# The boundary between two layers of a trunk kernel: a norm's sums, spread and use behind different products, the first pair's gate taken forward, keys and queries side by side

## The chip, the cores and the metric

The kernel runs on one core of a Trainium2 chip. Such a core has five engines that run at the same time, each through its own row of instructions in order, and wait for each other by semaphores: TensorE (PE in the profile, with PEld for its weight loads) does matrix products, VectorE (DVE), ScalarE (ACT) and GpSimd (POOL) work on tiles, and SyncE (SP) here issues the transfers between memory and the on-chip buffers. The metric is the device time of one execution in microseconds (us); shown is the median of the runs, beside a traced execution with the time of every instruction.

## The reference

The trunk has two layers. Each normalizes its input by rows, scales and shifts it by values computed from a condition `c`, runs a mixer, and adds the result times a gate. Layer 0's mixer is differential attention beside a recurrent unit; layer 1's is an attention in a window of a 16 x 64 grid, with 16 heads. The sequence has 1024 tokens of width 1024, one batch, all in fp32.

```python
def rms_norm(x, g):
    y = xf * lax.rsqrt(jnp.mean(xf * xf, axis=-1, keepdims=True) + EPS)
    return (y * g.astype(jnp.float32)).astype(x.dtype)
...
def odd_mixer(h, w_in, w_out, rpb):
    proj = h @ w_in
    q, k, v, g = jnp.split(proj, 4, axis=-1)
    out = neighborhood_attention(q.reshape(shp), k.reshape(shp), v.reshape(shp), rpb)
    return (out * jax.nn.silu(g)) @ w_out
...
    for l in range(DEPTH):
        mod = c_act @ ada_w[l] + ada_b[l]
        shift, scale, gate = jnp.split(mod, 3, axis=-1)
        h = rms_norm(x, norm_g[l]) * (1.0 + scale[:, None, :]) + shift[:, None, :]
        ...
        x = x + gate[:, None, :] * y
    return rms_norm(x, final_g)
```

## The kernel before

**Layout.** Activations stand transposed: channels on the partitions (8 tiles of 128, index `k` or `c`), tokens along the free axis, in two halves of 512 (`hf`). A product of fp32 numbers is made of three fast ones (`mm3`, L195 to L197): each operand is split into a high and a low part, and high x high, low activations x high weights and high activations x low weights are added up in PSUM (as the profile names them, L195, L196, L197).

**Weights.** They come in slabs of 1024 x 128, numbered in the order of use. SP loads a slab (`raw`, L152), ACT copies its high part (`whi`, L179), POOL subtracts for the low part (`wlo`, L180). `split_next` issues these two and then the load of the next slab, whose buffer comes free when the subtraction is done; `ahead(i)` does so early for slab `i`. `proj` (one product) takes a slab and one half: 24 matmuls, three for each `k`, the low weights first in the third. It yields after every two `k`, so that other work can be put between.

**The boundary.** `out_layer` with layer 0 makes the output projection, slabs 24 to 31 for the first half of the tokens and 32 to 39 for the second (`run`). Behind each slab an evacuation on DVE adds gate times product to x (L963), SP writes the sum to memory for later (L966), ACT squares it (L968) and DVE adds the square up (L974). `tail` then makes the norm: `ss_add` (L321) sums over the channels by 4 matmuls with ones, `rstd_rows` (L331 to L337) makes the reciprocal root on DVE in 11 steps, `spread` (L350) lays it out over all partitions (tile `bc`) by 4 matmuls, and `make_h` makes the next layer's input of each tile: L360 on DVE, the high part on ACT (L361), the low part on DVE (L362). For the first half the sums and the spread stood within the second half's products. For the second half the sums were made in two sets: of the first seven squares added up, and of the eighth.

Then come the first products of layer 1, head pair 0: keys (slab 40) and queries (slab 41), each for both halves, then values (slabs 42 and 43) and, among the attention's work, the gate (slab 44). Their evacuations are `evac_k` (L568 to L571), `evac_q` (L584 to L591, with two transfers that duplicate queries) and `evac_g1`, which takes tanh on ACT (L605) and multiplies on DVE (L606).

**Attention.** 64 units (8 pairs of heads, 2 halves, 4 blocks) go through three stages in a pipeline: `na_a` (logits `n`, L600 and L601; bias and maximum on DVE, L1162; exponential on ACT, L1165; division on POOL, L1170), `na_b` (transposes `etr`, L1182, copied by ACT and DVE, L1186 and L1188) and `na_c` (products with values, `no`, L1206). The projections of later pairs are fed in between by a feed that counts matmul time. The values of two pairs are made as a product of tokens x channels (`v`, L195 to L197, 128x256), copied out (`vt`), written to memory (`vd`, L1069) and read back in the window's order (`vc`, L1081). The bias of a unit is loaded by `load_bias` (L1137).

**Modulations.** The `c @ ada_w` rows for later use are made on DVE in between: `ada` pieces come by SP (L291), and L293 and L295 multiply and add them (`macc`). In layer 1 their buffers have the tag `tmp`, three in number, which the gate tiles `sg1` use too.

**What sets the order.** The program is written as generators that are advanced step by step (`some(gen, n)`); a list scheduler then orders the instructions of each engine by priority and readiness as it models them. `tc.high_priority()` takes instructions ahead, `tc.issue_after(x)` holds them behind instruction x. A tile that is allocated where another one lies waits for the last use of that one. SP is one queue in order for all loads and stores.

## Time and profile before

| quantity | value |
|---|---|
| median of 3 runs | 1241.4 us (1240.64 to 1245.04) |
| profiled execution, its time | 1242.87 us |
| its span (first to last instruction) | 1240.7 us |
| mean granted clock of PE | 0.983 of full speed |
| out projection of layer 0 to the last values' write | about 520 to 680 us |

"L12" is line 12 of the kernel's file. A row of a timeline has a start, a duration, engine, line, operation, output <- inputs and how many instructions it groups; in square brackets stands how long the engine stood idle before it and what ended that. A list of waits has the total, the number and the longest. The windows give busy time and count of each engine in a stretch. [...]

### The profile page before, as it was taken

The page shows a single profiled execution, that of the slowest core. Times are in us where ns is not written, and L with a number is a line of the kernel's source. Part 1 is how long each engine was busy: PE and PEld are TensorE (multiplying, and loading weights), DVE is VectorE, ACT ScalarE, POOL GpSimd, SP SyncE. Part 2 cuts the span into 40 slices and gives each one's busy share as a digit, 9 for nine tenths or more (in the row PEclk, how much of TensorE's full clock was granted, in tenths as well). Part 3 has the DMA queues.
Part 4 walks back from the last instruction along what each step waited for, and adds up shares of the span by engine and source line. Part 5 has one row for each costly group of instructions (what it writes and reads, how often), then busy time and mean ns, then how long its engine had stood idle before and what let it go on. Part 6 is the DMA issues. An engine that isn't in the chain of part 4 may idle for free.

```text
span 1240.7 us, 19096 instructions
## 1 busy us (share of the span) xinstructions
PE 1186.4 (96%) x7240; PEld 975.0 (79%) x7240; DVE 727.5 (59%) x1417; ACT 552.9 (45%) x1023; POOL 373.8 (30%) x348
## 2 busy tenths in 40 slices
PE   4989999899999999999999899999999999999997
PEld 3578877778888887777779689888988898877896
DVE  6753966798899889678561443353233324464344
ACT  4337658365656556423352333343243334465211
POOL 2114422133333325433322233233333333324100
PEclk8999999899999999999999899999999999999998
DMA  9511153222132201384433343333332333323312
GB/s 333 184 34 45 41 178 94 97 71 92 30 105 61 83 18 51 107 291 153 144 112 102 126 124 112 109 119 105 103 101 79 102 98 116 85 70 107 144 68 69
DMA packets 81467, 132.24 MB, mean 107 GB/s; under 512 B 7008, under 2 KB 48096, under 8 KB 81376
## 3 DMA queue, kind: packets, MB, share of 16 engines
q1 hardware_dynamic: 81376, 131.03, 33.6%
q8 instruction: 57, 0.93, 0.3%
q14 instruction: 34, 0.28, 0.1%
HBM read 110.03 MB, written 14.68 MB: 101 GB/s over the span
## 4 chain that ended last, share of the span: by engine, by line
PE 78%; DVE 10%; DMA 4%; issue 3%; ACT 2%; SPq 1%; POOL 1%; DVEq 0%; ACTq 0%; POOLq 0%
PE pp L195 15%; PE pp L197 15%; PE pp L196 15%; PE no L1206 4%; PE etr L1182 3%; PE v L195 2%; PE v L196 2%; PE atr L858 2%; PE v L197 2%; PE n L600 2%; PE n L601 2%; PE s L600 2%; PE s L601 2%; DMA vd<-vt 1%; DVE e L828 1%
## 5 line engine op out<-in xcount | busy, mean ns | idle before, releaser
L195 PE MATMUL pp<-ahi,whi 128*128 128x512 f32 (+1 forms) x1040 | 409.1, 394 | 3.3 <-DVE sgb L606 3.3
L197 PE MATMUL pp<-ahi,wlo 128*128 128x512 f32 (+1 forms) x1040 | 400.0, 385 | 0.8 <-POOL wlo L180 0.8
L196 PE MATMUL pp<-alo,whi 128*128 128x512 f32 (+1 forms) x1040 | 398.7, 384 | 0.0
L180 POOL TENSOR_TENSOR wlo<-raw,whi 128x1024 fp32r<-128x1024 f32 x80 | 195.6, 2447 | 332.8 <-ACT whi L179 332.8
L195 PEld LDWEIGHTS pp<-ahi,whi 128*128 128x128 f32 x1040 | 198.2, 191 | 46.3 <-issue 9.4
L197 PEld LDWEIGHTS pp<-ahi,wlo 128*128 128x128 f32 x1040 | 198.1, 190 | 39.7 <-POOL wlo L180 1.2
L196 PEld LDWEIGHTS pp<-alo,whi 128*128 128x128 f32 x1040 | 198.3, 191 | 33.4 <-issue 1.1
L179 ACT ACTIVATE whi<-raw 128x1024 fp32r<-128x1024 f32 x80 | 84.3, 1055 | 132.3 <-PE pp L196 84.1
L1162 DVE CUSTOM_DVE_ANT_0 e<-n,bias 128x288 f32<-128x288 f32 (+1 forms) x128 | 60.2, 505 | 141.2 <-PE n L601 75.3
L1170 POOL TENSOR_SCALAR e<-e,r 128x288 f32<-128x288 f32 (+1 forms) x128 | 70.1, 560 | 193.8 <-DVE r L1168 186.9
L1165 ACT ACTIVATE e<-e,nm 128x288 f32<-128x288 f32 (+1 forms) x128 | 72.8, 570 | 109.6 <-DVE nm L1162 108.9
L832 ACT ACTIVATE e<-e,nm 128x1024 f32<-128x1024 f32 x64 | 73.4, 1148 | 38.3 <-DVE nm L828 37.6
L828 DVE CUSTOM_DVE_ANT_0 e<-s,tb 128x1024 f32<-128x1024 f32 x64 | 76.9, 1217 | 4.0 <-DMA tb<-in_tb_dram 2.1
L196 PE MATMUL v<-wlo,ahi 128*128 128x256 f32 x256 | 72.5, 283 | 2.7 <-POOL wlo L180 2.7
L195 PE MATMUL v<-whi,ahi 128*128 128x256 f32 x256 | 74.7, 292 | 0.0
L197 PE MATMUL v<-whi,alo 128*128 128x256 f32 x256 | 72.3, 282 | 0.0
L295 DVE SCALAR_TENSOR_TENSOR macc<-ada,ctmp,macc 128x512 f32<-128x512 f32 x56 | 47.6, 851 | 28.7 <-DMA ada<-in_adaw_dram 28.3
L849 POOL TENSOR_SCALAR e<-e,r 128x256 f32<-128x256 f32 x32 | 32.9, 1027 | 100.6 <-DVE r L838 42.5
L1186 ACT ACTIVATE et<-etr 96x384 f32<-96x384 f32 (+1 forms) x64 | 31.2, 488 | 68.9 <-DVE et L1188 64.3
L1206 PE MATMUL no<-et,vc 96*64 96x128 f32 (+1 forms) x768 | 60.6, 282 | 0.0
L1206 PEld LDWEIGHTS no<-et,vc 96*64 96x64 f32 (+1 forms) x768 | 42.2, 136 | 21.6 <-issue 19.9
L963 DVE SCALAR_TENSOR_TENSOR xh<-pp,mod,xh 128x512 f32<-128x512 f32 (+1 forms) x40 | 25.6, 642 | 56.8 <-PE pp L197 49.5
(206 smaller groups left out, 2000.0 us busy)
## 6 DMA issues: line engine op xcount, KB each, us to landing
raw<-in_w_dram SPq DMA_DIRECT2D x56, 512.0 KB
ada<-in_adaw_dram SPq DMA_DIRECT2D x96, 256.0 KB
raw<-in_wo_dram SPq DMA_DIRECT2D x24, 512.0 KB
bias<-in_nab_dram SPq DMA_DIRECT2D x32, 288.0 KB
qq<-qq SPq DMA_DIRECT2D x48, 128.0 KB
bias<-in_nab_dram SPq DMA_DIRECT2D x16, 384.0 KB
xT<-in_xT_dram SPq DMA_DIRECT2D x16, 256.0 KB
xh<-in_xTp_dram SPq DMA_DIRECT2D x16, 256.0 KB
```

The lines of the kernel that those rows point to most:

```text
L179: A.activation(hi[:], raw[:], AF.Copy)
L180: G.tensor_tensor(lo[:], raw[:], hi[:], ALU.subtract)
L195: T.matmul(ps, lh, rh, start=start, stop=False)
L196: T.matmul(ps, lh, rl, start=False, stop=False)
L197: state["pe"] = T.matmul(ps, ll, rh, start=False, stop=stop).ins
L600: T.matmul(dst, qsel(q[m]), k, start=True, stop=False)
L828: state["dve"] = V.tensor_tensor_reduce(out=e[:], in0=ps[:].rearrange("p a b -> p (a b)"), in1=tbt[h][:, o:o + S], scale=-1.0, scalar=3.0e ...
L832: A.activation(e[:], e[:], AF.Exp, scale=-1.0, bias=nm[:], accum_out=sums[:, m:m + 1])
L1162: state["dve"] = V.tensor_tensor_reduce(out=e[:, m, :n], in0=ps[:, m, :n], in1=bias["now"][:, m, :n], scale=-1.0, scalar=3.0e38, op0=ALU.a ...
L1165: A.activation(e[:, m, :n], e[:, m, :n], AF.Exp, scale=-1.0, bias=nm[:, m:m + 1], accum_out=sums[:, m:m + 1])
L1170: state["pool"] = G.tensor_scalar(e[:, m, :n], e[:, m, :n], r[:, m:m + 1], 0.0, ALU.mult, ALU.add).ins
L1206: T.matmul(po[64 * m:64 * m + 64, b * P:(b + 1) * P], vch[p, b][:kn, j + hf, 64 * m:64 * m + 64], et[:kn, m, j * P:(j + 1) * P], start=(j ...
```

## The change

1. In `tail`, the sums and the spread are each held behind the last product that was issued before them (`issue_after(state["pe"])`). There is one more stop between `rstd_rows` and `spread`, so that another product can stand there. For layer 0 the eighth square is added on DVE and the second half has one set of sums.
2. The gate of pair 0 is made in the boundary, behind keys and queries of the first half. Slab numbers change: 42 is the gate, 43 and 44 the values. Its weights lie in buffers of `mixp[1]`, its tanh tiles in the boundary's pool `bp` under tag `sq`.
3. Order of the boundary: keys, first half; sums of the second half; queries, first half; spread; gate, first half, with `make_h` of the second half in between; keys and queries of the second half side by side, in pieces of six matmuls; gate, second half. The slabs are split earlier by more calls of `ahead`.

```diff
+        if i == at1["g", 0]:
+            pool, tags = mixp[1], ("mix6", "mix7")
...
-    def rstd_bc(ss, n, pool, bc):
-        spread(rstd_rows(ss, n, pool), bc)
...
-        order1 += vs + kq if p else kq + vs
-        if p < NA_PAIRS - 2:
+        order1 += vs + kq if p else kq + [("g", 0)] + vs
+        if 0 < p < NA_PAIRS - 2:
             order1.append(("g", p))
...
-                    last = s == len(segments) - 1
+                    last = l and s == len(segments) - 1
...
                 sums[s] = ss_start(f"ssl{l}_{s}")
-                ss_add(sums[s], acc[s], True, True, w)
+                with tc.issue_after(state["pe"]):
+                    ss_add(sums[s], acc[s], True, True, w)
+            if xdst is None:
+                rr = rstd_rows_act(sums[s], D, pool, w)
+            else:
+                rr = rstd_rows(sums[s], D, pool)
+                yield
             bc = ptp.tile([P, HF], F32, tag="pt", name=f"bc{l}_{s}")
-            if xdst is None:
-                spread(rstd_rows_act(sums[s], D, pool, w), bc, w)
-            else:
-                rstd_bc(sums[s], D, pool, bc)
+            with tc.issue_after(state["pe"]):
+                spread(rr, bc, w)
...
+    def evac_g1(p, pool, tag="sq", late=False):
+        def f(hf, ps):
+            c = slice(hf * HF, (hf + 1) * HF)
+            t = pool.tile([P, HF], F32, tag=tag, name="sg1", bufs=3)
+            ...
+                if hf == 0:
+                    mix_tile(p, f"sg1_{p}")
+                silu2(hf, ps, t, mixed[p][:, c])
...
         for c in range(KC):
             some(r1, 1)
-            some(t0, 2)
+            some(t0, (1, 1, 2, 2, 2, 2, 0, 0)[c])
         t1 = tail(1, to_h1)
+        ev = {"k": evac_k(("b", 0)), "q": evac_q(("b", 0)), "g": evac_g1(0, bp)}
+        first = lambda key, hf: proj(at1[key, 0], hf, ev[key], prep=False)
+        ahead(at1["q", 0])
+        some(first("k", 0), 99)
         some(t1, 1)
-        k0, q0 = evac_k(("b", 0)), evac_q(("b", 0))
-        for i, (key, hf, ev) in enumerate((("k", 0, k0), ("q", 0, q0), ("k", 1, k0), ("q", 1, q0))):
-            for _ in proj(at1[key, 0], hf, ev, prep=(i == 0)):
-                pass
-            some(t1, (3, 5, 0, 0)[i])
-        ahead(at1["q", 0] + 1)
+        ahead(at1["g", 0])
+        some(first("q", 0), 99)
+        some(t1, 1)
+        for _ in first("g", 0):
+            some(t1, 2)
+        k1, q1 = first("k", 1), first("q", 1)
+        for _ in range(5):
+            some(k1, 1)
+            some(q1, 1)
+        ahead(at1["g", 0] + 1)
+        some(first("g", 1), 99)
+        ahead(at1["g", 0] + 2)
...
-                t = ap.tile([P, HF], F32, tag="tmp", name="sg1", bufs=3)
...
+        feed.done.add("1g0")
...
-            if p < NA_PAIRS - 2:
-                feed.add(f"1g{p}", both(at1["g", p], evac_g1(p)))
+            if 0 < p < NA_PAIRS - 2:
+                feed.add(f"1g{p}", both(at1["g", p], evac_g1l(p)))
```

Lines below 340 shift by two, those of the attention by about 20: `mm3` is L197 to L199 now, the split L181 and L182, `spread` L352.

The first place is on PE, at the first half's spread (`bc0_0`). The names give slab and half of the product (`pp33_1` is slab 33, second half of the tokens), the activations' tile and the weights' parts. Before, it stood within slab 33's product:

```order
L195 MATMUL pp33_1_5303<-ahi1_1_4851,whi33_5266 128x512
L196 MATMUL pp33_1_5303<-alo1_1_4852,whi33_5266 128x512
L350 MATMUL bc0_0_5277<-rr_5279,sel_93 128x128 x4
L197 MATMUL pp33_1_5303<-ahi1_1_4851,wlo33_5267 128x512
L195 MATMUL pp33_1_5303<-ahi2_1_4855,whi33_5266 128x512
```

Now:

```order
L198 MATMUL pp33_1_5293<-alo3_1_4860,whi33_5266 128x512
L199 MATMUL pp33_1_5293<-ahi3_1_4859,wlo33_5267 128x512
L352 MATMUL bc0_0_5329<-rr_5278,sel_93 128x128 x4
L197 MATMUL pp34_1_5336<-ahi4_1_4831,whi34_5323 128x512
L198 MATMUL pp34_1_5336<-alo4_1_4832,whi34_5323 128x512
```

The spread moved from behind the 17th to behind the 24th matmul of slab 33. The second half's sums likewise stood within slab 39's and slab 40's products, its spread behind the 22nd matmul of slab 40; now the sums stand between slabs 40 and 41, the spread between slabs 41 and 42.

The second place is on POOL, the subtractions of the boundary's slabs. Before (40 keys, 41 queries, 42 and 43 values, 44 gate):

```order
L180 TENSOR_TENSOR wlo40_5603<-raw40_5567,whi40_5602 128x1024
L180 TENSOR_TENSOR wlo41_5659<-raw41_5606,whi41_5658 128x1024
L180 TENSOR_TENSOR wlo43_5860<-raw43_5811,whi43_5859 128x1024
L180 TENSOR_TENSOR wlo42_5808<-raw42_5662,whi42_5807 128x1024
L180 TENSOR_TENSOR wlo44_5932<-raw44_5863,whi44_5931 128x1024
```

Now (42 gate, 43 and 44 values):

```order
L182 TENSOR_TENSOR wlo40_5595<-raw40_5562,whi40_5594 128x1024
L182 TENSOR_TENSOR wlo42_5657<-raw42_5604,whi42_5656 128x1024
L182 TENSOR_TENSOR wlo41_5601<-raw41_5598,whi41_5600 128x1024
L182 TENSOR_TENSOR wlo43_5840<-raw43_5660,whi43_5839 128x1024
L182 TENSOR_TENSOR wlo44_5874<-raw44_5843,whi44_5873 128x1024
```

The gate's slab stands ahead of the queries' one, though the queries' product comes first on PE.

The third place is on SP, behind the boundary. Before, the last block of the values (`vd_83`) stood here, with only one `ada` load of layer 1 ahead of all value blocks:

```order
L152 DMA raw47_6330<-in_w1_dram 128x1024
L1069 DMA vd_83<-vt_6134 8x16x256
L152 DMA raw48_6485<-in_w1_dram 128x1024
L1081 DMA vc0_2_6147<-vd_83 128x1x128 x2
L1081 DMA vc0_3_6152<-vd_83 96x1x128 x2
L291 DMA ada_6206<-in_adaw_dram 128x512
L1137 DMA bias_6274<-in_nab_dram 128x2x384
L291 DMA ada_6271<-in_adaw_dram 128x512
```

Now, the first blocks of the values:

```order
L1157 DMA bias_5889<-in_nab_dram 128x2x288
L1157 DMA bias_5891<-in_nab_dram 128x2x384
L293 DMA ada_5998<-in_adaw_dram 128x512
L152 DMA raw47_6252<-in_w1_dram 128x1024
L1097 DMA vd_83<-vt_5950 8x16x256
L1157 DMA bias_6001<-in_nab_dram 128x2x288
L293 DMA ada_6268<-in_adaw_dram 128x512
L293 DMA ada_6334<-in_adaw_dram 128x512
L1097 DMA vd_83<-vt_5988 8x16x256
L1157 DMA bias_6271<-in_nab_dram 128x2x288
L293 DMA ada_6419<-in_adaw_dram 128x512
L1109 DMA vc0_0_6197<-vd_83 96x1x128
```

Four `ada` loads stand ahead of the first read of the values. The first two bias loads, which before stood ahead of slab 44's load, now stand behind slab 46's; the first of them waits for the gate's last multiply on DVE, since its tile lies where the boundary's pool was.

## The prediction

> **What bounds the kernel now.** I read the busy shares first, then the chain that ended last, the waits of PE around the boundary between the layers, and the windows of that stretch.

> ```profile
> span 1240.7 us, 19096 instructions
> PE 1186.4 (96%) x7240; PEld 975.0 (79%) x7240; DVE 727.5 (59%) x1417; ACT 552.9 (45%) x1023; POOL 373.8 (30%) x348
> PE 78%; DVE 10%; DMA 4%; issue 3%; ACT 2%; SPq 1%; POOL 1%; DVEq 0%; ACTq 0%; POOLq 0%
> ```

> PE is busy for 1186.4 of 1240.7 us, and 78% of the chain that ended last is its own matmuls. The change removes almost no matmul, so it can win only PE's idle time and the time that PE spends below full clock. The profiled execution took 1242.87 us, 2.17 us more than its span. My sum goes by that one; the median of the three runs, 1241.4, lies 1.5 us below it.

> PE's waits from 560 to 700 us, by what they waited for (total, how many, longest):

> ```profile
> PE etr L1182 <- ACT et L1186: 4.2, 1, 4.2
> PE v L196 <- POOL wlo L180: 2.7, 1, 2.7
> PE bc L350 <- DVE rr L337: 2.7, 2, 1.8
> PE ssl L321 <- DVE sq L974: 1.6, 1, 1.6
> PE etr L1182 <- POOL e L1170: 0.2, 1, 0.2
> ```

> Together 4.2 + 2.7 + 2.7 + 1.6 + 0.2 = 11.4 us. The windows show what follows such a wait (stretch, its length, busy us of PE, PEld, DVE, ACT and POOL with counts, granted clock, DMA share, GB/s):

> ```profile
> 573.50:576.90 3.40, 3.40 (x10) 2.61 (x9) 2.73 (x5) 1.93 (x3) 0.07 (x1) 0.50 0.00 0
> 576.90:607.20 30.30, 30.30 (x128) 23.97 (x127) 24.37 (x24) 12.73 (x18) 13.63 (x6) 1.00 0.54 179
> 641.80:645.20 3.40, 3.40 (x18) 3.40 (x17) 0.84 (x4) 1.87 (x4) 1.11 (x1) 0.50 0.97 289
> 689.60:696.40 6.80, 5.71 (x17) 4.72 (x18) 3.43 (x9) 3.56 (x8) 4.34 (x5) 0.50 0.33 101
> 696.40:1110.00 413.60, 413.60 (x2719) 347.75 (x2718) 164.52 (x430) 164.51 (x379) 128.56 (x151) 1.00 0.35 103
> ```

> At clock 1.00 a 128x512 matmul takes 30.30 / 128 = 0.237 us, a product of 24 so 5.7 us. In three stretches the clock is 0.50; they lose half of PE's busy time there, (3.40 + 3.40 + 5.71) / 2 = 6.3 us. After 696.4 PE has no idle time up to 1110, so a gain made before stays a gain.

> **The change part by part: what goes.**

> ```profile
> 572.14 1.16 PE L350 MATMUL bc<-rr,sel 128*128 128x128 f32 x8 [1.83 <-DVE rr L337]
> 609.22 0.43 PE L321 MATMUL ssl<-sq,ones 128*32 128x128 f32 x8 [1.65 <-DVE sq L974]
> 614.73 0.42 PE L321 MATMUL ssl<-sq,ones 128*32 128x128 f32 x8
> 619.72 1.13 PE L350 MATMUL bc<-rr,sel 128*128 128x128 f32 x8 [0.90 <-DVE rr L337]
> 640.99 0.39 PE L196 MATMUL v<-wlo,ahi 128*128 128x256 f32 x1 [2.74 <-POOL wlo L180]
> 690.69 1.49 PE L1182 MATMUL etr<-ident,e 128*96 128x128 f32 x6 [4.24 <-ACT et L1186]
> ```

> These rows are the waits of the view one by one. Waits 11.4 us, clock 6.3 us, and 0.4 us for one of the two sets of sum matmuls (609.22 and 614.73), of which one is left: if all of that went, 18.1 us.

> The 4.24 us wait needs a reason, since no line of the diff names it. It is DVE's:

> ```profile
> 688.74 0.75 DVE L295 SCALAR_TENSOR_TENSOR macc<-ada,ctmp,macc 128x512 f32<-128x512 f32 x1 [10.41 <-DMA ada<-in_adaw_dram]
> 647.80 0.72 SPq L1069 DMA_DIRECT2D vd<-vt  x1
> 677.33 0.61 SPq L1069 DMA_DIRECT2D vd<-vt  x1
> 682.48 2.44 SPq L1081 DMA_DIRECT2D vc<-vd  x4
> 684.96 0.47 SPq L291 DMA_DIRECT2D ada<-in_adaw_dram  x1
> ```

> DVE stood 10.41 us at the modulation step L295, whose `ada` load SP issued at 684.96, behind the last values written (677.33) and read back (682.48). PE's transposes `etr` wait for DVE's work behind that step. The load was late because its buffer (tag `tmp`) was held by the first pair's two gate tiles. After the change these lie in another pool, and in the changed order of SP four `ada` loads stand ahead of the `vc` loads instead of one. I count the wait and its half clock as gone: 4.24 + 5.71 / 2 = 7.1 us of the 18.1.

> **What comes.** PE gets to later work earlier, so the chains beside it become late.

> ```profile
> 566.67 2.39 POOL L180 TENSOR_TENSOR wlo<-raw,whi 128x1024 fp32r<-128x1024 f32 x1 [4.31 <-ACT whi L179]
> 566.71 2.44 DVE L332 TENSOR_SCALAR rr<-rs 128x128 int32<-128x128 int32 x1
> 571.79 0.29 DVE L337 SCALAR_TENSOR_TENSOR rr<-rt,rr 128x128 f32<-128x128 f32 x1
> ```

> First spread: `rr` still ends at 572.08. The spread now stands behind all 24 matmuls of slab 33 instead of 17, so 7 x 0.237 = 1.66 of its 1.83 us are filled. Left 0.2 to 0.4 us; I take 0.3. DVE's L332 is stretched to 2.44 us beside POOL's subtraction, and both stand side by side in the new order too, so I don't count on an earlier end.

> ```profile
> 590.19 1.04 ACT L179 ACTIVATE whi<-raw 128x1024 fp32r<-128x1024 f32 x1
> 591.31 2.45 POOL L180 TENSOR_TENSOR wlo<-raw,whi 128x1024 fp32r<-128x1024 f32 x1 [4.92 <-ACT whi L179]
> 594.01 0.40 PE L197 MATMUL pp<-ahi,wlo 128*128 128x512 f32 x1
> ```

> Slab 37: POOL's half ended at 593.76, and PE used it at 594.01 with 0.25 us to spare. PE will be there about 3.2 us earlier (1.83 - 0.3, and 3.4 / 2 of clock). ACT's split stands behind make_h work, which starts with the spread; only a part of it hangs on PE, so it comes forward less. I take two thirds, 2.1 us, so PE waits 3.2 - 2.1 - 0.25 = 0.85; I count 1.0. Bounds: 0 if the chain comes forward as much as PE, 2.4 if it hardly moves.

> ```profile
> 606.16 2.37 POOL L180 TENSOR_TENSOR wlo<-raw,whi 128x1024 fp32r<-128x1024 f32 x1 [3.37 <-ACT whi L179]
> 606.66 2.42 DVE L974 TENSOR_TENSOR sq<-sq 128x512 f32<-128x512 f32 x1 [0.70 <-ACT sq L968]
> 608.55 0.33 SPq L152 DMA_DIRECT2D raw<-in_w_dram  x1
> 562.30 0.68 DVE L974 TENSOR_TENSOR sq<-sq 128x512 f32<-128x512 f32 x1
> 638.66 0.34 SPq L152 DMA_DIRECT2D raw<-in_w_dram  x1
> 642.95 1.06 ACT L179 ACTIVATE whi<-raw 128x1024 fp32r<-128x1024 f32 x1 [3.41 <-DMA raw<-in_w_dram]
> 619.28 0.29 DVE L337 SCALAR_TENSOR_TENSOR rr<-rt,rr 128x128 f32<-128x128 f32 x1
> 609.20:638.00 28.80, 27.88 (x135) 21.62 (x135) 18.53 (x32) 12.14 (x18) 4.17 (x2) 1.00 0.24 73
> ```

> Second sum: it now waits for a square and an add that stand behind two splits on ACT, with slab 40's product of 5.7 us between the last evacuation and the sum. An add took 0.68 us undisturbed (562.30) and 2.42 beside POOL; 0.2 us left (bounds 0 to 1.7, the difference of these two). Spread of the second half: the chain of `rr` (4.4 us before, from the sums' end at 615.15 to 619.57) lies beside q0's product of 5.7 us: nothing.

> q0's low half: POOL now subtracts for the gate's slab 42 before q0's slab 41. Slab 42's `raw` goes out when slab 40's subtraction is done (608.55 in the old order) and lands some 3 to 4 us later (issued at 638.66, another was waited for until 642.95), then POOL takes twice 2.4 us, and q0's third matmul is due 5.7 us behind k0's start. By that I get 1.0 us; bounds 0 (the load lands early) and 2.4 (one whole subtraction more).

> Keys and queries side by side: they do the same 48 matmuls; DVE's three steps per tile keep up, since DVE was busy only 18.5 of the 28.8 us there. Nothing, at most 0.5. The splits of both value slabs now lie beside the gate's second half (5.7 us for 2 x 2.4): the 2.74 us are gone, as counted.

> The gate taken forward: 48 matmuls, 11.4 us, one load, one split, and two evacuations move out of the attention units, where they filled PE; PE's total is kept. The cover is PE's backlog of later projections; at the end of the attention the same number of fillers stands in the same order, so I cost it at nothing. If the cover failed, PE would show waits of the 0.2 us kind.

> Bias of the first unit: its memory is now held by the gate's tiles until the last gate multiply on DVE, so its load goes out later.

> ```profile
> 635.12 0.90 SPq L1137 DMA_DIRECT2D bias<-in_nab_dram  x2
> 643.89 0.46 DVE L1162 CUSTOM_DVE_ANT_0 e<-n,bias 128x288 f32<-128x288 f32 x1 [2.72 <-PE n L601]
> ```

> Before, 8 us passed from issue to use. Behind the wait stand SP's next loads and on DVE the unit's other steps; PE's first `etr` waits. Estimate 0.6 us (0.4 to 1.2), from a load's time of some 3 to 4 us against the 5.7 us of the first value products. The values' way through memory then follows it on SP: 0.5 us (0 to 1.5). Residue 0.1.

> Sum of what comes: 0.3 + 1.0 + 0.2 + 1.0 + 0.6 + 0.5 + 0.1 = 3.7 us. Span 1240.7 - 18.1 + 3.7 = 1226.3, time 1228.5; by the median 1227.0. **I forecast 1228.**

> [...] After waits of 1.83 and 2.74 us the clock was 0.50 for 3.4 us. [...]

> The add at 606.66 ended 0.55 us after POOL's subtraction, though it takes 0.68 alone. [...]

> **Rivals.** (1) The new waits reach the clock. A wait of 1.65 us cost no clock, one of 1.83 did. If slab 37 and q0 each wait some 2 us (the add caught between POOL's two subtractions costs 2.4), each costs 1.0 us more and 1.7 of clock: 1228.5 + 5.4 = 1233.9. For it: both chains have bounds of 2.4; against: both need their bad end. 0.17.
> (2) DVE's wait for `ada` stays or comes back at another load, since SP still queues all of them behind the value blocks: the 7.1 us stay, 1235. For it: eight blocks still lie between. Against: three loads more stand ahead. 0.10.
> (3) No new wait: 1228.5 - 3.7 = 1224.8. 0.07.
> (4) The halved clock has another cause than these waits, a drop at its own time, and two stretches of 3.4 us stay though the waits go: 1228.5 + 3.4 = 1231.9. Against: a drop follows each of the three longest waits and none of the shorter ones. [...] 0.05.
> (5) **Slower:** SP's one queue. The bias load waits for the gate multiply on DVE with the value blocks behind it; a block took (677.33 - 647.80) / 7 = 4.2 us. With 1.9 us more for each of eight blocks the gain is gone, with 2.7 more (8 x 2.7 = 21.6) the time is 1250. For it: the queue is in order; against: only the first blocks meet the bias loads. 0.03.

> **How the numbers follow.** Forecast 0.58, rivals 0.17, 0.10, 0.07, 0.05, 0.03. The range 1222 to 1236 takes in (1) to (4): (3) less the 1.5 us between profile and median and a little of the bounds gives 1222; (2) and the upper bounds of the waits give 1236. A measurement can tell about 0.5% from no change, 6.2 us. Faster by more means below 1235.2: forecast, (1), (3), (4) and a part of (2), less what the upper bounds take, 0.88; within 0.09; slower 0.03.

> **What would show it.** Right: no PE wait for `rr` above 0.5 us, one set of `ssl`, no half clock between 573 and 577 and behind the values' first product, no DVE wait for `ada` above 3 us, and small waits on `wlo` at slab 37 and q0. Wrong: a clock of 0.50 anywhere from 560 to 700, a wait of `no` for `vc`, or PE idle after 700.

## The result and the profile after

| | before | after |
|---|---|---|
| median | 1242.56 us (8 runs, 1239.54 to 1245.06) | 1229.45 us (8 runs, 1227.65 to 1237.81) |
| ratio after/before | | 0.9908, 95% interval 0.9889 to 0.9926 |
| profiled execution, time / span | 1242.87 / 1240.7 us | 1229.11 / 1227.2 us |
| mean granted clock | 0.983 | 0.995 |

The forecast was 1228, the range 1222 to 1236. The medians lie 13.1 us apart; the ratio makes it 11.4 us (9.2 to 13.8 by its interval). The page of the changed kernel, its span, busy shares and chain:

```profile
span 1227.2 us, 19073 instructions
PE 1177.9 (96%) x7232; PEld 969.2 (79%) x7232; DVE 725.6 (59%) x1418; ACT 553.5 (45%) x1023; POOL 376.3 (31%) x348
PE 82%; DVE 10%; DMA 3%; ACT 2%; POOL 1%; issue 1%; SPq 0%; DVEq 0%; ACTq 0%; POOLq 0%
```

PE's share of that chain is 82% (before 78%). PE's waits from 560 to 700 us in the changed kernel:

```profile
PE etr L1202 <- POOL e L1190: 2.2, 1, 2.2
PE pp L199 <- POOL wlo L182: 1.0, 1, 1.0
PE bc L352 <- DVE rr L339: 0.2, 1, 0.2
```

The rows of its timeline that carry them, with the sums among them:

```profile
571.91 1.16 PE L352 MATMUL bc<-rr,sel 128*128 128x128 f32 x8 [0.16 <-DVE rr L339]
612.93 0.43 PE L323 MATMUL ssl<-sq,ones 128*32 128x128 f32 x8
615.06 0.50 PE L199 MATMUL pp<-ahi,wlo 128*128 128x512 f32 x1 [1.04 <-POOL wlo L182]
651.71 1.52 PE L1202 MATMUL etr<-ident,e 128*96 128x128 f32 x6 [2.25 <-POOL e L1190]
```

All five waits whose rows the prediction shows are gone but for 0.16 us of the first spread, and there is one set of sums at 612.93. Two waits are new: 1.04 us for the queries' low weights (forecast 1.0) and 2.25 us at the first unit's transposes (forecast 0.6). From 560 to 700 PE waits 3.4 us instead of 11.4, 8.0 us less. The rest is clock. Windows of the changed kernel, the second behind the 2.25 us wait; the first lies outside the change, behind a wait of 2.04 us at the first layer's attention (`obc`):

```profile
515.88:519.30 3.42, 3.42 (x19) 2.92 (x20) 1.44 (x2) 0.63 (x1) 0.00 (x0) 1.00 0.50 153
652.21:655.62 3.41, 3.30 (x15) 3.25 (x15) 0.62 (x2) 0.80 (x3) 1.23 (x3) 0.50 0.81 265
```

The same place in the kernel before, behind the same wait of 2.05 us:

```profile
515.09:518.77 3.68, 3.68 (x13) 3.20 (x14) 1.44 (x2) 0.33 (x1) 0.00 (x0) 0.55 0.44 142
```

So the changed kernel still loses 3.30 x 0.50 = 1.65 us to the clock in its boundary, where the kernel before lost 6.3. Both figures, and the losses named below, count half of PE's busy time at 0.50, which is an estimate. Shown in the kernel before is the time from one 128x512 matmul's start to the next, at 0.50 and at 1.00:

```profile
692.40 0.63 PE L196 MATMUL pp<-alo,whi 128*128 128x512 f32 x1
...
695.82 0.63 PE L195 MATMUL pp<-ahi,whi 128*128 128x512 f32 x1
...
579.88 0.40 PE L195 MATMUL pp<-ahi,whi 128*128 128x512 f32 x1
...
582.76 0.40 PE L195 MATMUL pp<-ahi,whi 128*128 128x512 f32 x1
```

The first two stand 8 matmuls apart, 0.43 us each, the other two 12 apart, 0.24 us each. By that 44% of the busy time is lost, 1.45 us of the 3.30 and 5.5 us where 6.3 is counted. And at `obc`, which the change does not touch, the kernel before lost 3.68 x 0.45 = 1.7 us and this execution none: that part of the difference is not the change's (the stretch ahead of `obc` took 0.8 us longer in the changed kernel, 515.88 against 515.09, so that 0.9 us are left of it). Waits 8.0, clock in the boundary 4.6, one set of sums 0.4 make 13.0; with the 0.9 it is 13.9, against the span's 13.5 us.

### The profile page after: what moved, and what is told of

Its sections match the earlier page's. It is cut to its first block, busy times and chain, and to the rows that moved or that the text cites. A ratio compares the mean times of both kernels' runs of the same rounds, so it can differ in the third digit from the quotient of the medians.

```text
span 1227.2 us, 19073 instructions
## 1 busy us (share of the span) xinstructions
PE 1177.9 (96%) x7232; PEld 969.2 (79%) x7232; DVE 725.6 (59%) x1418; ACT 553.5 (45%) x1023; POOL 376.3 (31%) x348
## 4 chain that ended last, share of the span: by engine, by line
PE 82%; DVE 10%; DMA 3%; ACT 2%; POOL 1%; issue 1%; SPq 0%; DVEq 0%; ACTq 0%; POOLq 0%
PE pp L197 16%; PE pp L199 16%; PE pp L198 15%; PE no L1226 4%; PE etr L1202 3%; PE v L197 3%; PE v L198 2%; PE v L199 2%; PE atr L857 2%; PE s L599 2%; PE s L600 2%; PE n L599 2%; PE n L600 2%; PE o L198 1%; PE o L197 1%
## 5 line engine op out<-in xcount | busy, mean ns | idle before, releaser
L197 PE MATMUL pp<-ahi,whi 128*128 128x512 f32 (+1 forms) x1040 | 405.9, 390 | 3.7 <-DVE sgb L605 3.3
L199 PE MATMUL pp<-ahi,wlo 128*128 128x512 f32 (+1 forms) x1040 | 397.4, 382 | 2.5 <-POOL wlo L182 2.5
L182 POOL TENSOR_TENSOR wlo<-raw,whi 128x1024 fp32r<-128x1024 f32 x80 | 196.1, 2454 | 333.5 <-ACT whi L181 330.0
L197 PEld LDWEIGHTS pp<-ahi,whi 128*128 128x128 f32 x1040 | 196.3, 189 | 45.8 <-issue 9.6
L199 PEld LDWEIGHTS pp<-ahi,wlo 128*128 128x128 f32 x1040 | 196.3, 189 | 41.1 <-POOL wlo L182 3.4
L1182 DVE CUSTOM_DVE_ANT_0 e<-n,bias 128x288 f32<-128x288 f32 (+1 forms) x128 | 60.4, 504 | 151.8 <-PE n L600 76.7
L181 ACT ACTIVATE whi<-raw 128x1024 fp32r<-128x1024 f32 x80 | 84.3, 1055 | 133.4 <-PE pp L198 88.2
L197 PE MATMUL v<-whi,ahi 128*128 128x256 f32 x256 | 74.7, 292 | 0.0
L199 PE MATMUL v<-whi,alo 128*128 128x256 f32 x256 | 72.3, 282 | 0.0
L864 ACT ACTIVATE ath<-atr 128x512 fp32r<-128x512 f32 x64 | 38.0, 596 | 45.7 <-PE atr L857 45.4
```

What stands on the lines that cost most here:

```text
L181: A.activation(hi[:], raw[:], AF.Copy)
L182: G.tensor_tensor(lo[:], raw[:], hi[:], ALU.subtract)
L197: T.matmul(ps, lh, rh, start=start, stop=False)
L199: state["pe"] = T.matmul(ps, ll, rh, start=False, stop=stop).ins
L1182: state["dve"] = V.tensor_tensor_reduce(out=e[:, m, :n], in0=ps[:, m, :n], in1=bias["now"][:, m, :n], scale=-1.0, scalar=3.0e38, op0=ALU.a ...
```

## The experiments

**Is the `ada` wait due to the held buffers?** In the kernel before, only the gate's tanh is moved out of the `tmp` buffers:

```diff
-                t = ap.tile([P, HF], F32, tag="tmp", name="sg1", bufs=3)
+                t = ap.tile([P, HF], F32, tag="tmp", name="sg1", bufs=3) if p else None
...
-                    silu2(hf, ps, t, mixed[p][:, c])
+                    silu2(hf, ps, t if p else mixed[0][:, c], mixed[p][:, c])
```

> The kernel before, with one edit: the first pair's gate takes its tanh into the gate's own tile instead of a buffer of the tag tmp; the order of the products is the one before. Theory (buffers held): DVE's wait of 10.41 us for ada goes, and PE's wait of 4.24 us at etr with it; if the half clock behind it goes too, 7.1 us faster than before (ratio about 0.9943), without it 4.2 us (0.9966). Rival (the queue): SP queues the ada loads behind the value blocks whatever holds the buffers; the DVE wait stays above 5 us and the time within 1 us of before. For the clock: the wait at the layer-0 attention's obc near 515 us is in all kernels alike (2.05 us before, with clock 0.50 behind it; 2.04 us in the changed kernel, with clock 1.00). If a wait's length alone decides, it is one or the other in all of these runs; if something else decides, some runs show it and some don't.

Measured: 1234.41 us (10 runs) against 1240.04 for before, ratio 0.9963 (0.9944 to 0.9982). The longest of PE's waits from 560 to 700:

```profile
PE bc L350 <- DVE rr L337: 2.8, 2, 1.8
PE v L196 <- POOL wlo L180: 2.7, 1, 2.7
PE ssl L321 <- DVE sq L974: 1.6, 1, 1.6
PE etr L1182 <- POOL e L1170: 0.8, 1, 0.8
```

The windows behind two of them, 1.82 us at the first spread and 2.73 us at the first value product:

```profile
574.09:577.50 3.41, 3.41 (x19) 2.92 (x20) 2.22 (x4) 1.44 (x2) 0.00 (x0) 1.00 0.00 0
642.18:646.00 3.82, 3.82 (x30) 3.82 (x30) 1.06 (x6) 1.66 (x4) 0.52 (x1) 1.00 0.96 287
```

The wait for `ada` is gone though SP still has the value blocks: the buffers held it. A single tile's place is worth 0.37% of the kernel, 4.6 us (2.2 to 6.9 by the interval). And the waits of 1.82 and 2.73 us, the same as in the kernel before, are followed by a clock of 1.00.

**The bias load behind the gate's tile.** The same edit of the tanh in the changed kernel.

> The changed kernel, with one edit: the gate's tanh goes into the gate's own tile, so no tile of the boundary's pool is held by the gate. Theory: the first unit's bias load (issued at 644.45) waited for the gate's last multiply; it now goes out by 641 or earlier, DVE's wait of 4.78 us for it ends, PE's wait of 2.25 us at the first etr falls under 0.5 us, and the time by 2.3 to 4.0 us against the changed kernel (2.25 of wait, 1.7 of half clock), about 1226 us. Rival: the load is held by another tile of that pool or is late in the queue; the wait stays above 1.5 us and the time is that of the changed kernel within 1 us.

Measured: 1228.51 us (1227.46 to 1230.34). From its timeline, PE's first transposes, and DVE's and ACT's rows ahead of them:

```profile
650.34 1.01 PE L1202 MATMUL etr<-ident,e 128*96 128x128 f32 x6 [1.74 <-POOL e L1190]
...
645.05 0.46 DVE L1182 CUSTOM_DVE_ANT_0 e<-n,bias 128x288 f32<-128x288 f32 x1 [1.54 <-PE n L600]
647.44 0.69 DVE L605 SCALAR_TENSOR_TENSOR sg<-sg,pp 128x512 f32<-128x512 f32 x1 [1.92 <-ACT sg L604]
...
645.72 1.06 ACT L181 ACTIVATE whi<-raw 128x1024 fp32r<-128x1024 f32 x1 [3.83 <-DVE nm L1182]
646.81 0.60 ACT L604 ACTIVATE sg<-pp 128x512 f32<-128x512 f32 x1
647.30 0.53 ACT L1185 ACTIVATE e<-e,nm 128x288 f32<-128x288 f32 x1
```

DVE no longer waits for the bias (1.54 us for PE's logits instead of 4.78 for the load), yet PE's wait is still 1.74 us. ACT now copies slab 45 ahead of the gate's tanh and of the first exponential, and DVE's gate multiply stands between the first two maxima. The load went out at 636.73, as the theory has it, so the rival has the numbers right and the cause not: a second reason lay behind the first. Nor is the 1.74 us a gain: the unedited changed kernel, traced once more below, shows the same 1.74, with DVE's wait for the bias at 4.27 us.

**The queries' low weights.** The subtraction of the gate's slab held behind that of the queries' slab, on POOL alone:

```diff
-        with tc.high_priority() if j < 2 else tc.issue_after(state["pool"]):
+        with (tc.issue_after(state["sub"]) if i == at1["g", 0] else
+              tc.high_priority() if j < 2 else tc.issue_after(state["pool"])):
             A.activation(hi[:], raw[:], AF.Copy)
-            G.tensor_tensor(lo[:], raw[:], hi[:], ALU.subtract)
+            state["sub"] = G.tensor_tensor(lo[:], raw[:], hi[:], ALU.subtract).ins
```

> The changed kernel, with one edit: the split of the gate's slab 42 is held behind the split of the queries' slab 41 on POOL. Theory: PE's wait of 1.04 us in the queries' product is due to POOL's order; it falls under 0.3 us and the time by 1.0 us, about 1228.4 us. Rival: slab 41 has its weights late for another reason, or the wait moves to the gate's product, which comes 5.7 us later; the sum of PE's waits for wlo between 600 and 640 stays above 0.8 us.

Measured: 1228.35 us (1227.63 to 1230.58), the time that was expected, though not by the way expected. POOL's two subtractions, ACT's two copies, DVE's add of the last square, and PE's sums and spread:

```profile
611.01 5.19 POOL L183 TENSOR_TENSOR wlo<-raw,whi 128x1024 fp32r<-128x1024 f32 x2 [5.63 <-ACT whi L182]
...
608.93 2.01 ACT L182 ACTIVATE whi<-raw 128x1024 fp32r<-128x1024 f32 x2 [5.46 <-DMA raw<-in_w_dram]
...
611.49 2.47 DVE L974 TENSOR_TENSOR sq<-sq 128x512 f32<-128x512 f32 x1 [2.93 <-ACT sq L968]
...
614.11 0.43 PE L324 MATMUL ssl<-sq,ones 128*32 128x128 f32 x8 [0.89 <-DVE sq L974]
620.79 1.13 PE L353 MATMUL bc<-rr,sel 128*128 128x128 f32 x8 [0.60 <-DVE rr L340]
```

The wait for the low weights is gone, and waits of 0.89 and 0.60 us at the sums and the second spread stand in its place. Together that is more than the 1.04 us that went, so the match of the time was luck. ACT still copied slab 42 first, whose load it had to wait for, so POOL started at 611.01, just ahead of DVE's add at 611.49. The add takes 0.68 us alone; here 2.47, until 613.96, which is 0.55 us behind the end of the first subtraction (611.01 + 2.4). The add ahead of it in the same trace, begun at 603.50 beside a subtraction of 2.39 us from 603.00, likewise took 2.43 us and ended 0.54 us behind that subtraction's end. Then the same with ACT's copy held as well:

```diff
+        held = i == at1["g", 0]
+        with (tc.issue_after(state["copy"]) if held else ...):
+            state["copy"] = A.activation(hi[:], raw[:], AF.Copy).ins
```

> The changed kernel with slab 42's copy on ACT and its subtraction on POOL both behind slab 41's, nothing else. Theory: with POOL's order alone, POOL had to wait for ACT, which copied slab 42 first, and the subtraction then blocked DVE's add of the last square; with ACT's order too, POOL starts some 2 us earlier, and no wait over 0.3 us is left at the queries' product, the sums or the second spread; etr's wait stays at 1.6 to 2.3 us. Rival: the add is blocked by the second subtraction all the same, and the sums wait 0.5 us or more.

Its subtractions and its add:

```profile
606.49 5.19 POOL L186 TENSOR_TENSOR wlo<-raw,whi 128x1024 fp32r<-128x1024 f32 x2 [3.37 <-ACT whi L183]
...
608.27 1.16 DVE L977 TENSOR_TENSOR sq<-sq 128x512 f32<-128x512 f32 x1 [1.99 <-ACT sq L971]
```

PE's waits from 560 to 700:

```profile
PE etr L1206 <- POOL e L1194: 2.1, 1, 2.1
```

POOL starts 1.78 us ahead of the add, which takes 1.16 us instead of 0.68 and ends at 609.43, again 0.54 us behind the first subtraction's end (606.49 + 2.4) and ahead of the second's (611.68). The wait at `etr` is the only one left in the list. One execution took 1225.43 us; with one there is no interval.

**Both new waits together, in two forms.** First the edits of the second and third experiment in one kernel:

> Both edits of the two kernels before this one. Theory: their gains add up, 2.25 + 1.04 = 3.3 us without the clock and up to 5.0 with it; 1224.5 to 1226.2 us. Rival: with the earlier loads the next one in SP's queue is late (the values' blocks, bias or ada of a later unit) and PE waits there for over 1 us; the gain is under 2 us.

Measured: 1228.16 us (1226.4 to 1229.12). 0.9 us at the sums, 0.6 at the second spread and 1.8 at the transposes are left: the waits moved within the boundary, and the gain is under 2 us. That is the rival's number, but not its cause, a late load in SP's queue. Then with the reasons found above: slab 42 behind slab 41 on both engines, the tanh in its own tile, slab 45's copy behind the last tanh and its subtraction without priority:

```diff
+              tc.issue_after(state["tanh"]) if i == at1["g", 0] + 3 else
...
+              tc.issue_after(state["pool"]) if i == at1["g", 0] + 3 and "pool" in state else
```

> The changed kernel with its two new waits attacked on each engine: slab 42's copy on ACT and subtraction on POOL both behind slab 41's; the gate's tanh in the gate's own tile; slab 45's copy on ACT behind the gate's last tanh, its subtraction on POOL without priority, so that the first units' divisions go first. Theory: the queries' wait of 1.04 us goes without a wait at the sums in its place (POOL starts 1.2 us earlier than in the kernel with POOL's order alone), and etr's wait of 2.25 us falls to 0.3 to 1.0 us (ACT's exponential still stands behind slab 45's load); 2.3 to 3.0 us less wait, time 1225.5 to 1227. Rival: the waits move again (sums, spread, a later unit) and the sum of PE's waits from 600 to 660 stays over 2.5 us; time within 1 us of the changed kernel.

PE's waits from 560 to 700:

```profile
PE bc L358 <- DVE rr L345: 0.2, 1, 0.2
```

That is the whole list. 1225.89 us (1225.11 to 1226.92), ratio to before 0.9874 (0.9858 to 0.9890), below the medians of the kernel before and of the changed one. It was run once more beside the changed kernel on one chip:

> The changed kernel, unchanged, beside the next one on the same chip: 1227.5 to 1231 us. Waits of 1.0 us at the queries' product and 1.5 to 2.3 us at the first etr; half clock behind the latter or not.

> The kernel with both new waits mended, unchanged from the run before: 1225 to 1227 us, 2.5 to 4.5 us less than the changed kernel on the same chip, if its gain is the two waits (3.3 us) and at times a half clock; if the gain was only the clock's chance, the two are within 1.5 us of each other.

1227.21 us (1225.62 to 1228.99; ratio 0.9896, 0.9881 to 0.9912) for the changed kernel and 1225.35 us (1223.89 to 1226.59; 0.9881, 0.9864 to 0.9898) for the mended one. The medians differ by 1.9 us, between the two expectations (2.5 to 4.5, and under 1.5), and the intervals overlap: that the waits are gone is shown by the traces, what this is worth in time is not settled. In these two traces PE's waits from 560 to 700 are 1.03 and 1.74 us in the one and 0.16 to 0.34 us each in the other, apart from 1.33 us at 560 for the last modulation row, which the mending doesn't touch.

**Which part carries the gain?** The gate put back into the feed. Its tanh lies in a `tmp` buffer again, and the order of the slabs is the one before; sums, spread and keys beside queries are as in the change:

```diff
-        order1 += vs + kq if p else kq + [("g", 0)] + vs
-        if 0 < p < NA_PAIRS - 2:
+        order1 += vs + kq if p else kq + vs
+        if p < NA_PAIRS - 2:
...
-        ahead(at1["g", 0])
         some(first("q", 0), 99)
         some(t1, 1)
-        for _ in first("g", 0):
-            some(t1, 2)
+        some(t1, 8)
...
-        ahead(at1["g", 0] + 1)
-        some(first("g", 1), 99)
-        ahead(at1["g", 0] + 2)
+        ahead(at1["q", 0] + 1)
...
-            if 0 < p < NA_PAIRS - 2:
+            if p < NA_PAIRS - 2:
                 feed.add(f"1g{p}", both(at1["g", p], evac_g1l(p)))
```

> The changed kernel with the first pair's gate put back into the feed (its tanh again in a tmp buffer, slab order as before); sums, spread and keys beside queries as in the change. Theory (the gate is the cover): PE waits about 4 us in all between the second half's spread and the end of keys and queries, since DVE's make_h of eight tiles took from 621.3 to 635.2 and only 11.4 us of products lie beside it; the wait of about 2.7 us at the first value product and of about 4.2 us at etr for ada come back; 11 us of waits and up to 5 of clock, time 1238 to 1244. Rival (the norm's new places carry the gain): the waits named stay under 3 us in all, time under 1234.

Measured: 1240.37 us (10 runs) against 1241.32, ratio 0.9994 (0.9979 to 1.0010): nothing left. The longest of PE's waits from 560 to 700:

```profile
PE etr L1195 <- ACT et L1199: 4.4, 1, 4.4
PE v L196 <- POOL wlo L180: 3.4, 1, 3.4
PE pp L195 <- ACT ahi L358: 1.6, 1, 1.6
PE pp L196 <- DVE alo L359: 0.6, 1, 0.6
```

The waits at the sums and both spreads are gone in this kernel too, but a wait of 1.6 + 0.6 us behind the second spread (half of what I expected) and 3.4 instead of 2.7 us at the values pay for it, and the `ada` wait is back. Two things were put back here, the gate's place and its tanh's buffer. The `ada` wait of 4.4 us (DVE stands 10.6 us for the load again) belongs to the buffer, which the first experiment freed without moving the gate; the other 5.6 us of waits, with 3.22 us of PE's work at 0.50 behind the 1.6 us (623.66 to 627.08, 1.6 us lost), stand for the cover. The mean clock of this execution was 0.981, that of the kernel before 0.983. No run has the gate in the feed with its tanh outside `tmp`, so the two shares are read from the trace and not from times.

**The first spread alone put back** inside slab 33's product, with `make_h` advanced as before:

```diff
-            some(t0, (1, 1, 2, 2, 2, 2, 0, 0)[c])
+            some(t0, 2)
...
-            with tc.issue_after(state["pe"]):
+            if xdst is None or s:
+                with tc.issue_after(state["pe"]):
+                    spread(rr, bc, w)
+            else:
                 spread(rr, bc, w)
```

> The changed kernel with the first half's spread back inside slab 33's product (behind its 17th matmul), and make_h of the first half advanced as before; the rest as in the change. Theory: PE's wait for rr comes back, 1.6 to 1.9 us at about 570, with or without 1.7 us of half clock; time 1.7 to 3.4 us above the changed kernel. Rival: the wait moves to another place behind it (the split of slab 37, or a sum), where the changed kernel has none, and the sum of PE's waits from 565 to 615 differs by over 1 us from the first spread's wait alone.

```profile
571.64 0.82 PE L352 MATMUL bc<-rr,sel 128*128 128x128 f32 x5 [1.84 <-DVE rr L339]
592.58 0.51 PE L199 MATMUL pp<-ahi,wlo 128*128 128x512 f32 x1 [0.40 <-POOL wlo L182]
```

1230.45 us (1229.46 to 1232.08), 1.0 us over the changed kernel instead of the 1.7 to 3.4 expected, and within the scatter of both (ratio to before 0.9911, the changed kernel's 0.9908). The wait is back with its full 1.84 us, and 0.40 us at slab 37 with it; no half clock follows here. That the first spread's place matters is shown by the trace, not by the time.

**Keys, then queries:**

```diff
-        for _ in range(5):
-            some(k1, 1)
-            some(q1, 1)
+        some(k1, 99)
+        some(q1, 99)
```

> The changed kernel with the second half's keys advanced to their end ahead of the queries, not in pieces side by side. Theory (as the prediction has it): DVE keeps up in either order; no wait over 0.5 us between 626 and 640, the time of the changed kernel within 1 us. Rival: side by side gives make_h its time; its last low part ended at 635.2, and keys alone would need it at 632, so PE waits 1 to 3 us in the keys' product.

1228.94 us (1227.96 to 1231.17), and no wait between 626 and 640. The scheduler put the queries' first matmuls among the keys' by itself, so this shows only that the written order does not matter here.

**The clock once more:** the kernel before, unchanged.

> The kernel before, unchanged, for one more look at its clock. Theory (phase decides): PE's waits of about 1.8, 1.65, 2.7 and 4.2 us are there again, but the half clock behind the first and the third isn't the same as in the first look (then 1.7 us behind each); behind 4.2 us it is there. Rival (length decides): 1.7 us lost behind the 1.8 and the 2.7 us wait again, none behind 1.65.

Its windows behind the waits of 1.84, 1.65 and 2.74 us:

```profile
570.44:574.00 3.56, 3.56 (x19) 3.07 (x20) 2.37 (x4) 1.58 (x2) 0.00 (x0) 1.00 0.00 1
606.70:610.10 3.40, 3.40 (x21) 2.62 (x22) 0.00 (x0) 0.00 (x0) 0.00 (x0) 1.00 0.45 154
638.47:645.00 6.53, 6.53 (x29) 6.53 (x30) 1.03 (x6) 2.21 (x5) 2.37 (x1) 0.53 0.80 234
```

Nothing is lost behind 1.84 us, and 6.53 x 0.47 = 3.1 us behind 2.74, where the first trace had 1.7. So the same waits cost another amount this time, as the theory has it. One execution took 1239.33 us.

## Why the prediction was right

The time lies 1.5 us above the forecast. By its steps:

- **The waits that go:** 1.83, 1.65, 0.90, 2.74, 4.24 us, each gone to 0.16 or less, as reckoned. That the 4.24 us hung on the `tmp` buffers is shown by the first experiment.
- **First spread:** 0.3 forecast, 0.16 measured; 1.83 less the 1.66 that the prediction reckons as filled is 0.17.
- **Slab 37:** 1.0 forecast, none measured; this step failed. ACT's copy of slab 37 came 3.78 us earlier, not 2.1:

```profile
586.41 1.04 ACT L181 ACTIVATE whi<-raw 128x1024 fp32r<-128x1024 f32 x1
```

  It was at 590.19 before, and PE's use came 3.39 us earlier (590.62 against 594.01), so the chain kept ahead of it. I had taken two thirds of PE's lead for a chain whose order I didn't follow row by row. The change's other schedule of `make_h` (1, 1, 2, 2, 2, 2, 0, 0) seems to be why: with the old one, in the kernel with the first spread put back, a wait of 0.40 us is there, and one of 0.4 us also in the two traces of the old order without half clock ahead of it (the first experiment and the second trace of the kernel before). No run changes the schedule alone.
- **Second sum and spread:** 0.2 and 0 forecast, none measured. How near the edge they stand shows in the third experiment, where POOL began 0.48 us ahead of the add instead of 1.42 (609.83 against 611.25 in the changed kernel), which turned them into 0.89 and 0.60.
- **Queries' low weights:** 1.0 forecast, 1.04 measured, by the order named. The load of slab 42 went out at 605.19 and ACT copied it at 608.69, 3.5 us later, as reckoned. That it is 1.0 to so little is partly luck, since the bounds were 0 and 2.4. What I had not named is that ACT's order, too, makes it.
- **First bias:** 0.6 forecast with 1.2 as the upper bound, 2.25 measured (1.74 in the second trace of the changed kernel). The mechanism was right, the size not: the load went out at 644.45, when the gate's last multiply was done, and took 4.75 us:

```profile
643.74 0.69 DVE L605 SCALAR_TENSOR_TENSOR sg<-sg,pp 128x512 f32<-128x512 f32 x1 [1.65 <-ACT sg L604]
644.45 0.90 SPq L1157 DMA_DIRECT2D bias<-in_nab_dram  x2
649.20 0.46 DVE L1182 CUSTOM_DVE_ANT_0 e<-n,bias 128x288 f32<-128x288 f32 x1 [4.78 <-DMA bias<-in_nab_dram]
```

- **The values' way:** 0.5 forecast, no wait at `no` measured. New waits in all: 3.7 forecast, 3.4 measured. Slab 37, the second sum and the values' way were put 1.7 us too high and the first bias 1.65 too low, so that the sum agrees by luck.
- **The clock:** 6.3 us counted as gone, with "a wait of 1.65 us cost no clock, one of 1.83 did". This reasoning failed. The half of PE's busy time in the 6.3 us is not shown by any run: a 128x512 matmul took 0.43 us at 0.50 against 0.24 at 1.00, which makes it 5.5 us. In the two traces of the kernel before and that of its edit, the waits of the first spread and of the first value product cost 3.4, 3.1 (all of it behind the 2.74 us of the second trace) and 0 us, so part of what I counted was the chance of one execution; in the changed kernel the 2.25 us wait lost 1.65 us. A new wait that reaches the clock is what rival 1 feared, at another place than it named. Rival 4, a cause apart from these waits, was not right either: every drop in the boundary stands behind a wait. The last section says which waits are followed by one.
- **The cover:** the prediction costs the gate at nothing, which held but for one wait of 0.4 us behind 700 us. What it doesn't say is that nearly all depends on the gate's place: the ratio to before is 0.9994 with the gate in the feed and 0.9908 with it in the boundary. The other parts move waits; the gate's 11.4 us of matmuls give them something to hide behind, and its early place frees the `tmp` buffers, which is the largest single part in the trace (7.1 us with its half clock; 4.6 by the first experiment's time).
- **Its own signs:** of those that it lists as wrong, two came: a clock of 0.50 within 560 to 700, at 652.21, and PE idle behind 700, by 0.4 us. The time was right all the same, since both are small.

## What to carry to other kernels

When a wait is removed by moving it behind other work, ask which product stands at the new place: without the gate's 48 matmuls there, and with its tanh back in the held buffers, the same edits gained nothing. Look at what holds a buffer before blaming the queue that loads it; one tile's place was worth 4.6 us. A new order of two splits has to be set on every engine that touches them, or the wait only changes its name.

## What the runs showed of the hardware

The same wait is not followed by a halved clock in every trace. At `obc`, in the first traces of ten kernels (all but the one with the split's order set on both engines), PE waits 2.04 to 2.05 us; behind it the 128x512 matmuls start 0.43 us apart, at a clock of 0.50, in eight of them, and 0.24 us apart, at 1.00, in two, the changed kernel and the one with the first spread put back. The wait of 1.82 to 1.84 us at the first spread had a clock of 0.50 behind it in the first trace of the kernel before, and 1.00 in its second trace, in the first experiment and with the first spread put back. The wait of 2.73 to 2.74 us at the first value product had 0.50 behind it in the first trace of the kernel before (641.77 to 645.19), a mean of 0.53 over the 6.53 us from 638.47 in its second, and 1.00 in the first experiment. And in the kernel with keys ahead of queries, a wait of 1.6 us at `etr` was followed by a mean of 0.64 over the 4.71 us from 651.29.

```profile
512.07:515.48 3.41, 1.36 (x8) 0.81 (x7) 2.89 (x3) 0.39 (x1) 2.35 (x1) 1.00 0.00 0
515.48:518.89 3.41, 3.41 (x13) 2.93 (x13) 1.44 (x2) 0.45 (x1) 0.00 (x0) 0.50 0.48 154
```

In the changed kernel:

```profile
512.26:515.67 3.41, 1.59 (x7) 0.93 (x5) 3.27 (x5) 1.00 (x1) 2.33 (x1) 1.00 0.00 0
515.67:519.09 3.42, 3.21 (x18) 2.77 (x19) 1.60 (x3) 0.44 (x1) 0.01 (x1) 1.00 0.50 153
```

In the one the whole wait of 2.05 us lies in a step; in the other the step ends 0.21 us before the wait does, 1.83 us are left in it, and the clock stays at 1.00. The wait of 2.73 us in the first experiment was split by the grid of that trace into 1.17 and 1.56 us and cost nothing. The grid lies differently against the same wait in different traces: the one of 2.04 to 2.05 us at `obc` ends 0.39 us ahead of a step's end in the kernel before and 0.21 us behind one in the changed kernel. Behind a wait that may halve the clock, reckon with a mean over executions, not with one trace's loss.
